# A gated activation bound by DMA: swapping the load and store queues, four-row activations, and the first load and first store cut into four transfers by partition

## The chip, the cores and the metric

The kernel runs on one core of one Trainium2 chip. DMA engines move the data between HBM, the chip's large memory, and SBUF, its on-chip memory, in which every tile here lies across 128 partitions. ACT (ScalarE) and DVE (VectorE) are the engines that compute here; SP only issues transfers here. A transfer *lands* when its data has arrived. The metric is device time in microseconds (us); a few rounds of the kernel before and of the other kernel alternate on one chip. All runs quoted with a ratio were in the fast state, with a granted clock of 1.0. A ratio is the mean time of one kernel's fast runs over the mean of the other's fast runs of the same rounds, so it is not quite the ratio of the medians quoted beside it.

## The reference

```python
# x: (32, 512, 2048) float32
x1, x2 = x[..., :1024], x[..., 1024:]
out = (x1 * (1 / (1 + np.exp(-x1)))) * x2        # (32, 512, 1024) float32
```

134.2 MB are read, 67.1 MB are written, and little is computed in between.

## The kernel before

There are 16 tiles of 1024 rows. A partition holds 8 consecutive rows of x, which are 64 KB in one piece in HBM, and 32 KB of output. Input tile `xt` and output tile `ot` have two buffers each. Loads are issued on ACT's queue, stores on SP's.

```python
K = 8; KC = 2
in_pool  = ctx.enter_context(tc.tile_pool(name="in_pool", bufs=2))
out_pool = ctx.enter_context(tc.tile_pool(name="out_pool", bufs=2))

def load(i):
    xt = in_pool.tile([P, K, in_cols], dt, name="xt")
    nc.scalar.dma_start(out=xt[:, :plan[i][1], :], in_=view(x_flat, i))
    loaded[i] = xt

load(0)                       # moved ahead of the first barrier
load(1)
for i in range(n_tiles):
    # ... xt, ov, ot, last
    for c in range(0, k, KC):
        # ot[c:ce] = Silu(xt[c:ce, :half]) on ACT
        # ot[c:ce] *= xt[c:ce, half:]      on DVE
        if last:
            nc.sync.dma_start(out=ov[:, c:ce, :], in_=ot[:, c:ce, :])
    if not last:
        nc.sync.dma_start(out=ov, in_=ot[:, :k, :])
    if i + 2 < n_tiles:
        load(i + 2)
```

## Time and profile before

| | before |
|---|---|
| time, median of 3 runs | 470.97 us (470.84 to 471.04) |
| span of the profiled run | 468.9 us |
| DVE busy, ACT busy | 142.3 us, 118.2 us |
| bytes moved, mean rate | 201.35 MB, 429 GB/s |

These are lines of the page of the kernel before: busy time of each engine with its share of the span; the DMA share in 40 slices (9 is 90% or more); the two DMA queues with packets, MB and share of the 16 DMA engines; and the chain of waits, by engine and by line.

```profile
DVE 142.3 (30%) x64; ACT 118.2 (25%) x65; POOL 0.2 (0%) x4
...
DMA  9899999999999998999999999999999989999998
...
q10 hardware_dynamic: 2304, 134.22, 66.4%
q1 hardware_dynamic: 2736, 67.11, 33.2%
...
DMA 80%; DVE 15%; ACT 3%; DVEq 0%; issue 0%
DMA xt<-in_x_dram 80%; DVE ot L92 15%; ACT ot L87 3%; DVEq L128 0%
```

No compute engine is busy for a third of the time, while DMA is busy in every slice: DMA is the bound. In the chain the DMA part is all loads (`xt<-in_x_dram`): a tile's compute starts when its load lands. The view of waits of the kernel before says the same (microseconds in total, times, longest):

```profile
ACT ot L87 <- DMA xt<-in_x_dram: 338.8, 16, 22.1
```

Two stretches of the kernel before, the start and the middle (columns: stretch, length, busy time of each engine, granted clock, DMA share, GB/s):

```profile
0.00:28.00 28.00, 4.18 (x2) 7.41 (x5) 0.20 (x4) 1.00 0.97 412
60.00:434.00 374.00, 115.65 (x52) 95.01 (x52) 0.00 (x0) 1.00 1.00 433
```

The trace holds a record of every DMA packet: start, duration, size, queue. It doesn't name the engine; the packets fall into sixteen chains, in each of which a packet starts where another ends, and a chain is taken for an engine. A load is 128 packets of 64 KB, eight for each of the 16 DMA engines; a store is 128 packets of 32 KB. In the steady part a load packet takes 2.418 us and a store packet 1.213 us, and each engine goes from one packet to the next without a gap (of 3696 steps between 60 and 434 us over 99% have none, and the longest is 0.32 us). 64 KB in 2.418 us is 27.1 GB/s an engine, or 434 GB/s for sixteen. The 433 GB/s that the view gives for the middle stretch agrees.

### The profile page before, as it was taken

The page shows a single profiled execution, that of the slowest core. Times are in us where ns is not written, and L with a number is a line of the kernel's source. Part 1 is how long each engine was busy: PE and PEld are TensorE (multiplying, and loading weights), DVE is VectorE, ACT ScalarE, POOL GpSimd, SP SyncE. Part 2 cuts the span into 40 slices and gives each one's busy share as a digit, 9 for nine tenths or more (in the row PEclk, how much of TensorE's full clock was granted, in tenths as well). Part 3 has the DMA queues.
Part 4 walks back from the last instruction along what each step waited for, and adds up shares of the span by engine and source line. Part 5 has one row for each costly group of instructions (what it writes and reads, how often), then busy time and mean ns, then how long its engine had stood idle before and what let it go on. Part 6 is the DMA issues. An engine that isn't in the chain of part 4 may idle for free.

```text
span 468.9 us, 269 instructions
## 1 busy us (share of the span) xinstructions
DVE 142.3 (30%) x64; ACT 118.2 (25%) x65; POOL 0.2 (0%) x4
## 2 busy tenths in 40 slices
DVE  0070705106061160601507025070250702407034
ACT  1142406023060330603206032060420604106051
POOL 0000000000000000000000000000000000000000
DMA  9899999999999998999999999999999989999998
GB/s 431 375 447 403 447 447 447 403 419 431 447 447 403 447 492 363 442 492 391 458 403 439 456 447 403 409 442 447 447 403 444 467 386 447 442 419 481 400 409 354
DMA packets 5042, 201.35 MB, mean 429 GB/s; under 512 B 560, under 2 KB 560, under 8 KB 560
## 3 DMA queue, kind: packets, MB, share of 16 engines
q10 hardware_dynamic: 2304, 134.22, 66.4%
q1 hardware_dynamic: 2736, 67.11, 33.2%
q14 instruction: 2, 0.02, 0.0%
HBM read 134.22 MB, written 67.11 MB: 429 GB/s over the span
## 4 chain that ended last, share of the span: by engine, by line
DMA 80%; DVE 15%; ACT 3%; DVEq 0%; issue 0%
DMA xt<-in_x_dram 80%; DVE ot L92 15%; ACT ot L87 3%; DVEq L128 0%
## 5 line engine op out<-in xcount | busy, mean ns | idle before, releaser
L92 DVE TENSOR_TENSOR ot<-ot,xt 128x2048 f32<-128x2048 f32 x64 | 142.3, 2286 | 319.5 <-ACT ot L87 319.5
L87 ACT ACTIVATE ot<-xt 128x2048 f32<-128x2048 f32 x64 | 116.9, 1897 | 338.8 <-DMA xt<-in_x_dram 338.8
L87 ACT ACT_TABLE_LOAD x1 | 1.3, 1283 | 1.3 <-PEq L117 1.3
L117 POOL MEMSET const-uint8-127<- 128x1 uint8 x1 | 0.1, 102 | 0.0
L117 POOL MEMSET const-bfloat16-1.0<- 128x1 bf16 x1 | 0.1, 101 | 0.0
L117 POOL MEMSET const-float32-0.0<- 128x1 f32 x1 | 0.1, 98 | 0.2 <-issue 0.2
L117 POOL MEMSET const-float32-1.0<- 128x1 f32 x1 | 0.1, 98 | 0.0
## 6 DMA issues: line engine op xcount, KB each, us to landing
out_dram<-ot SPq DMA_DIRECT2D x15, 4096.0 KB, 39.8
out_dram<-ot SPq DMA_DIRECT2D x4, 1024.0 KB, 5.7
xt<-in_x_dram ACTq DMA_DIRECT2D x16, 47.1
```

The lines of the kernel that those rows point to most:

```text
L87: nc.scalar.activation(out=ot[:, c:ce, :], in_=xt[:, c:ce, :half], func=mybir.ActivationFunctionType.Silu,)
L92: nc.vector.tensor_mul(out=ot[:, c:ce, :], in0=ot[:, c:ce, :], in1=xt[:, c:ce, half:],)
L117: nc = _bacc.Bacc("TRN2", target_bir_lowering=False, num_devices=1)
```

## The change

The intent, as far as the code tells: start each DMA queue sooner by giving it a small first transfer (one partition for each DMA engine), and halve the number of ACT and DVE instructions.

```diff
-    K = 8
-    KC = 2
+    K = 8
+    KC = 4
+    KC_LAST = 2
+    STARTING = [slice(0, None, 8), slice(4, None, 8), slice(2, None, 4), slice(1, None, 2)]
...
+    def start_ring(queue, dst, src, split):
+        for ps in STARTING if split else [slice(None)]:
+            queue.dma_start(out=dst[ps], in_=src[ps])
...
-        nc.scalar.dma_start(out=xt[:, :plan[i][1], :], in_=view(x_flat, i))
+        start_ring(nc.sync, xt, view(x_flat, i), split=i == 0)
...
+        if i < n_tiles - 1:
+            for c in range(0, K, KC):
+                silu(ot, xt, c, c + KC)
+                mul(ot, xt, c, c + KC)
+            start_ring(nc.scalar, ov, ot, split=i == 0)
+            if i + 2 < n_tiles:
+                load(i + 2)
+            continue
+        # last tile: two rows at a time, each store issued two activations later, on nc.scalar
```

All four parts of the first load, instead of one load, are moved ahead of the first barrier.

More of the change, by code (lines that the diff above doesn't have):

```diff
@@ L6, with issue_ahead_of_the_first_barrier @@
 from concourse._compat import with_exitstack
-def issue_ahead_of_the_first_barrier(nc):
+def issue_ahead_of_the_first_barrier(nc, count):
     head, body = nc.main_func.blocks[:2]
-    load = next(ins for ins in body.instructions if type(ins).__name__ == "InstDMACopy")
+    loads = [ins for ins in body.instructions if type(ins).__name__ == "InstDMACopy"][:count]
     at = next(
         j for j, ins in enumerate(head.instructions)
-        if ins.engine == load.engine and type(ins).__name__ == "InstDrain"
+        if ins.engine == loads[0].engine and type(ins).__name__ == "InstDrain"
     )
-    body.instructions = [ins for ins in body.instructions if ins.name != load.name]
-    head.instructions = head.instructions[:at] + [load] + head.instructions[at:]
+    names = {ins.name for ins in loads}
+    body.instructions = [ins for ins in body.instructions if ins.name not in names]
+    head.instructions = head.instructions[:at] + loads + head.instructions[at:]
 @with_exitstack
@@ L63, in view @@
         return flat[row0:row0 + P * k].rearrange("(p k) d -> p k d", k=k)
-    nc.at_finalize(issue_ahead_of_the_first_barrier)
+    nc.at_finalize(lambda nc: issue_ahead_of_the_first_barrier(nc, len(STARTING)))
     ctx.enter_context(tc.manual_schedule())
+    def start_ring(queue, dst, src, split):
+        for ps in STARTING if split else [slice(None)]:
+            queue.dma_start(out=dst[ps], in_=src[ps])
     loaded = {}
@@ L73, in load, with silu, mul @@
         xt = in_pool.tile([P, K, in_cols], dt, name="xt")
-        nc.scalar.dma_start(out=xt[:, :plan[i][1], :], in_=view(x_flat, i))
+        start_ring(nc.sync, xt, view(x_flat, i), split=i == 0)
         loaded[i] = xt
+    def silu(ot, xt, c, ce):
+        nc.scalar.activation(
+            out=ot[:, c:ce, :],
+            in_=xt[:, c:ce, :half],
+            func=mybir.ActivationFunctionType.Silu,
+        )
+    def mul(ot, xt, c, ce):
+        nc.vector.tensor_mul(
+            out=ot[:, c:ce, :],
+            in0=ot[:, c:ce, :],
+            in1=xt[:, c:ce, half:],
+        )
     load(0)
@@ L79 @@
     for i in range(n_tiles):
-        k = plan[i][1]
         xt = loaded.pop(i)
-        last = i == n_tiles - 1
         ov = view(out_flat, i)
         ot = out_pool.tile([P, K, half], dt, name="ot")
-        for c in range(0, k, KC):
-            ce = min(c + KC, k)
-            nc.scalar.activation(
-                out=ot[:, c:ce, :],
-                in_=xt[:, c:ce, :half],
-                func=mybir.ActivationFunctionType.Silu,
-            )
-            nc.vector.tensor_mul(
-                out=ot[:, c:ce, :],
-                in0=ot[:, c:ce, :],
-                in1=xt[:, c:ce, half:],
-            )
-            if last:
-                nc.sync.dma_start(out=ov[:, c:ce, :], in_=ot[:, c:ce, :])
-        if not last:
-            nc.sync.dma_start(out=ov, in_=ot[:, :k, :])
-        if i + 2 < n_tiles:
-            load(i + 2)
+        if i < n_tiles - 1:
[6 more added lines that the diff above has]
+            continue
+        cuts = list(range(0, K, KC_LAST))
+        for n, c in enumerate(cuts + [None, None]):
+            if c is not None:
+                silu(ot, xt, c, c + KC_LAST)
+                mul(ot, xt, c, c + KC_LAST)
+            if n >= 2:
+                b = cuts[n - 2]
+                nc.scalar.dma_start(out=ov[:, b:b + KC_LAST, :], in_=ot[:, b:b + KC_LAST, :])
 _INS = ['x']
```

## The prediction

> **What bounds the kernel now.** The 16 DMA engines. The engine table gives DVE 142.3 us and ACT 118.2 us of 468.9; the slices show DMA busy at 8 to 9 tenths throughout; the DMA view gives 201.35 MB at a mean of 429 GB/s. [...] (a 64 KB load packet takes 2.418 us on one engine, so 434 for sixteen). In the packet records the engines work back to back from 1.14–1.84 us to 466.8–467.6 us, with no gap over 0.4 us. At 434 GB/s the bytes need 464 us (an estimate), so only about 5 us is not steady transfer:
> - start: the first packet begins 1.0 us after the first load is issued at 0.13 us, and the 16 first packets take 2.5–3.4 us, mostly 0.6–0.9 too long;
> - first store: issued at 32.75 us, and at 35.65–36.0 us every engine has one load packet of 3.2–3.4 us, 0.85 us too long. No later store shows this. Both are the first use of a queue;
> - end: 1.3 us from the last packet to the last instruction.
>
> **What the change does.**
> 1. Split first load and first store: the first transfer is 16 partitions, one descriptor per engine instead of eight. [...] Estimate: 0.5–1.0 us off the start and 0.4–0.8 off the first store, on all engines at once, so on the critical path. Cost: three more issues each (0.33–0.38 us in the timeline), hidden behind the 2.4 us packets.
> 2. Loads on SP, stores on ACT: same engines, same bytes. At most 0.1 us at the start (SP's first instruction is at 0.00 us, ACT's at 0.13).
> 3. Four-row activations: from ACT 1.9 us and DVE 2.29 us for two rows, a tile takes about 12.5 us instead of 10.8. Store and next load are issued 1.7 us later, but a load is already queued (8.4 MB, over 19 us), so DMA doesn't idle: worth 0. Fewer fixed costs on ACT and DVE: worth 0.
> 4. Last tile: stores issued two activations later, on ACT. After the last load lands (451.0 us) DMA works 16.1 us more, of which 9.7 us are the last tile's stores; 6.4 us of older stores cover the wait for the first. The last store still goes when the last multiply ends, with about 3 us of slack. Worth 0.
>
> **Predicted.** 470.97 − 1.3 = 469.7 us, range 468.7 to 472.5. Faster by over 2%: 0.01; within 2%: 0.93; slower by over 2%: 0.06.
>
> **What would show it.** The first 64 KB packets take 2.4–2.7 us; no packet near 35 us takes over 3 us; total DMA bytes and the 2.418 us steady packet unchanged; ACT and DVE busy time fall by several us without effect; DMA is still about 80% of the chain of waits; the span falls by 1 to 1.6 us.
>
> **What would make it wrong.** The partitions of the split transfers. [...] If sixteen engines take one partition each, [...] packets of about 4.8 us (store: 2.4), some 5 us lost on the load and 2.5 on the store; if the bigger parts collide as well, up to 19 and 10 us, slower by over 2%. No run here shows it yet; I take it to be unlikely[...]. Also, if the stall is a fixed cost of waking a queue, the split gains nothing: 471.0.

No number of the sum is cut: 470.97 − 1.3 = 469.7 us. The 1.3 us is about the middle of the two estimates of step 1 taken together (0.5–1.0 and 0.4–0.8 us), and these come from the first packets and the load packet at the first store, 0.6–0.9 and 0.85 us too long in the trace. That a smaller first transfer shortens them was an assumption and not shown. In the risk, 4.8 and 2.4 us are an estimate, twice the 2.418 and 1.213 us of the trace.

## The result, and the profile after

| | before | after |
|---|---|---|
| time, median of 6 runs | 471.0 us (470.71 to 471.12) | 483.85 us (483.66 to 484.75) |
| ratio, 95% interval | | 1.0278 (1.0265 to 1.0291) |
| span of the profiled run | 468.9 us | 482.1 us |
| DVE busy, ACT busy | 142.3 us, 118.2 us | 140.3 us, 115.4 us |

The change makes the kernel 2.8% slower. The same lines of the page of the changed kernel:

```profile
DVE 140.3 (29%) x34; ACT 115.4 (24%) x35; POOL 0.2 (0%) x4
...
DMA  9999999999999999999999999999999999999997
...
q1 hardware_dynamic: 2352, 134.22, 66.9%
q10 hardware_dynamic: 2784, 67.11, 32.4%
...
DMA 77%; DVE 14%; ACT 6%; DVEq 0%; ACTq 0%; SPq 0%; issue 0%
DMA out_dram<-ot 71%; DVE ot L95 14%; ACT ot L88 6%; DMA xt<-in_x_dram 5%; DVEq L149 0%; ACTq L78 0%; SPq L78 0%; ACT L88 0%; ACTq L88 0%
```

Here is a trap for the reader: DMA is as busy as before and moves the same bytes, so the busy shares show nothing wrong. What changed is how long the same packets take, and what the chain is made of. Its DMA part is now stores (`out_dram<-ot` 71%), where it was loads. The view of waits of the changed kernel:

```profile
ACT ot L88 <- DMA out_dram<-ot: 314.4, 14, 23.3
ACT L88 <- DMA xt<-in_x_dram: 27.3, 1, 27.3
ACT ot L88 <- DMA xt<-in_x_dram: 12.1, 1, 12.1
```

ACT waits 14 times for a store, because the output buffer it wants to write is still being stored when its input has landed. The same two stretches of the changed kernel:

```profile
0.00:28.00 28.00, 0.00 (x0) 0.74 (x1) 0.20 (x4) 1.00 0.98 337
60.00:434.00 374.00, 105.26 (x25) 85.47 (x24) 0.00 (x0) 1.00 1.01 427
```

So there are two losses, both at a DMA share of about 1: the first 28 us move 337 GB/s instead of 412, and the middle moves 427 instead of 433. The packet records say where. The mean load packet goes from 2.430 to 2.519 us; with 128 of them on each engine that is 11.4 us. Of the time above 2.418 us, 5.5 us an engine lie in the first load (before: 0.6) and 7.4 us after 60 us (before: 0.0). Most of the rest of the 13.2 us is imbalance: the engines finish between 476.98 and 480.96 us instead of between 466.81 and 467.62, and the slowest counts.

The first three packets of one engine of each kernel (start, duration in us; then the range of all sixteen engines):

```
before, first load:  1.14 3.15 | 4.29 2.42 | 6.70 2.42    first packets 2.47 to 3.44, then 2.42
after,  first load:  1.38 4.29 | 5.67 4.95 | 10.62 3.28   first packets 4.29 to 5.29, second 4.94 to 4.96, third 2.66 to 3.28, then 2.42
```

The two 16-partition transfers run at half rate (4.94 to 4.96 us for the second packet, against 2.42). Tile 0 lands at 27.17 us instead of 21.86.

The middle loss is spread over all tiles. Number a load's eight packets on an engine L0 to L7. From the third tile on, L1 is on average 0.16 us and L2 0.32 us too long, all others together about 0.05. The sequence of packets on one engine, near 200 us (`s` is a store packet, `#` a packet of 4 bytes that takes 9 ns, the number is ns above 2418):

```
before:  ... L4 s L5 # L6 s L7 s # s L0 s L1 s L2 ...
after:   ... L6 s L7 s # s L0 # L1 s L2+384 s L3 s L4 ...
```

Each engine has one `#` at the end of each transfer: the two queues hold 560 of them in the kernel before (35 transfers on 16 engines) and 656 in the changed one (41 transfers). In these records loads and stores alternate packet by packet, and a `#` stands in the sequence like a packet of its queue: between 60 and 434 us of the kernel before, 3680 of 3696 pairs of neighbours on an engine change the queue if the `#` is counted, and 2864 of 3280 if it isn't. So beside a store's `#` two loads follow each other, and beside a load's `#` two stores. Before, the store's `#` comes first and the load's 7.3 us later. After, the load's comes first and the store's 3.6 us later. The order of the two endings has flipped, and it stays so for the rest of the run.

### The profile page after: what moved, and what is told of

It reads as the page before. It is cut to its first block, busy times and chain, and to the rows that moved or that the text cites. A ratio compares the mean times of both kernels' runs of the same rounds, so it can differ in the third digit from the quotient of the medians.

```text
span 482.1 us, 219 instructions
## 1 busy us (share of the span) xinstructions
DVE 140.3 (29%) x34; ACT 115.4 (24%) x35; POOL 0.2 (0%) x4
## 4 chain that ended last, share of the span: by engine, by line
DMA 77%; DVE 14%; ACT 6%; DVEq 0%; ACTq 0%; SPq 0%; issue 0%
DMA out_dram<-ot 71%; DVE ot L95 14%; ACT ot L88 6%; DMA xt<-in_x_dram 5%; DVEq L149 0%; ACTq L78 0%; SPq L78 0%; ACT L88 0%; ACTq L88 0%
## 5 line engine op out<-in xcount | busy, mean ns | idle before, releaser
L95 DVE TENSOR_TENSOR ot<-ot,xt 128x4096 f32<-128x4096 f32 (+1 forms) x34 | 140.3, 4170 | 332.4 <-ACT ot L88 332.4
L88 ACT ACTIVATE ot<-xt 128x4096 f32<-128x4096 f32 (+1 forms) x34 | 114.1, 3407 | 326.5 <-DMA out_dram<-ot 314.4
```

What stands on the lines that cost most here:

```text
L88: nc.scalar.activation(out=ot[:, c:ce, :], in_=xt[:, c:ce, :half], func=mybir.ActivationFunctionType.Silu,)
L95: nc.vector.tensor_mul(out=ot[:, c:ce, :], in0=ot[:, c:ce, :], in1=xt[:, c:ce, half:],)
```

## The experiments

Fifteen kernels ran, in four groups, each beside the kernel before (medians 471.41, 471.37, 470.91 and 471.35 us in turn). All but three gave the right result. Executions of the runs with slow loads differ by up to 5 us (o from 480.04 to 485.06); why was not looked into.

The main theory had two parts by the end. The **collision theory**: in the 16-partition transfers some partitions that are moved at the same moment slow each other. The **order theory**: load packets are slow in every tile when the stores of a tile end after the next load has landed. The rivals were the distance of the rows in HBM, small transfers as such, the swap of the queues, the uneven engines that the split leaves, and the split store in itself.

### One part at a time

**a_load_split**: the kernel before with the load split alone (all four parts ahead of the first barrier, as in the changed kernel).

```diff
-        nc.scalar.dma_start(out=xt[:, :plan[i][1], :], in_=view(x_flat, i))
+        for ps in STARTING if i == 0 else [slice(None)]:
+            nc.scalar.dma_start(out=xt[ps], in_=view(x_flat, i)[ps])
```

> The kernel before with only its first load split in four (still on ACT). Collision theory: the two 16-partition transfers of the first load run at half rate, so tile 0 lands about 5.3 us later than before's 21.9 us, and that cost is there whatever else is changed: about 476 us from this alone. Spread theory for the other 7.5 us of the loss: the split leaves the 16 DMA engines 0.7 us apart instead of 0.35, and that spread grows and slows later loads; then this run loses them too and takes 480 to 484 us, with the spread at a landing growing from 0.7 to over 4 us. Phase theory: the slow loads come from where the first store's packets fall between the load packets; here compute and store start relative to the load packets about as before, so about 476 us and a spread that stays under 1.5 us.

Measured 475.17 us, ratio 1.0082 (1.0067 to 1.0097). Tile 0 landed at 27.4 us; the load packets after 60 us were all at 2.42 us, although the engines were 0.7 to 1.6 us apart. So the load split costs about 4 us, and engines as uneven as these don't by themselves slow the later loads. The split wins a little back: the stall at the first store, 0.9 us on each engine, is gone here. Why is open.

**b_store_split**: the kernel before with the store split alone.

```diff
-            nc.sync.dma_start(out=ov, in_=ot[:, :k, :])
+            for ps in STARTING if i == 0 else [slice(None)]:
+                nc.sync.dma_start(out=ov[ps], in_=ot[ps])
```

> The kernel before with only its first store split in four (still on SP). In the changed kernel the first store's packets took 1.21 to 1.58 us against 1.21, and no load packet near it stalled by 0.85 us as in the kernel before. Start-of-queue theory: this run loses the 0.85 us stall and is 0.5 to 0.9 us faster than before, about 470.3 us. Collision theory applied to stores: [...] store packets of about 2.4 us, 2 to 10 us slower. Phase theory: if the earlier start of store packets shifts the store tiles against the load tiles by a slot, later loads may slow by some us.

The 2.4 us for the collision is an estimate, twice the 1.213 us of a store packet.

Measured 470.95 us, ratio 0.9994 (0.9977 to 1.0011): the same. The load packet at the first store took 3.35 to 3.48 us, as against 3.18 to 3.42 before. So the stall doesn't shrink with the size of the first store, and step 1 of the prediction fails here. Stores and loads now end together (the store 0.01 us later), where the stores ended 7.3 us earlier before. The three added transfers put three more `#` into the store queue of each engine; if a load packet of 2.418 us goes beside each, that makes 7.3 us (an estimate). The view of waits:

```profile
ACT ot L88 <- DMA out_dram<-ot: 302.8, 14, 21.8
```

**c_no_split**: the changed kernel with `STARTING = [slice(None)]`, so neither is split.

> The changed kernel with neither transfer split: loads on SP, stores on ACT, four-row activations, later stores in the last tile. Collision theory with spread theory: no collision, no spread, so the time of before, 470 to 472 us. Queue theory (the swap of the two queues slows the later loads): about 478 us, loads of over 2.5 us in every tile. Phase theory: the first store comes 1.7 us later, so the store tiles may lie one slot (3.6 us) nearer to the load tiles; if so some loads in every tile are slow and it takes 472 to 479 us, and then the four-row run on the kernel before must show the same.

Measured 471.27 us, ratio 1.0003 (0.9985 to 1.0020): the same. Stores end 3.6 us before the next load. The swap of queues and the later stores of the last tile cost nothing.

**d_four_rows**: the kernel before with four-row activations in all tiles but the last (`kc = KC if last else 4`).

> The kernel before with four-row activations in all tiles but the last, nothing else. Queue theory and spread theory: as before, 471 us within 0.5. Phase theory: the store tiles come 1.7 us later against the load tiles; if the landing of a store moves from 7.3 us to about 3.6 us before the next load's landing, slow loads (over 2.5 us) appear in every tile and the time is 472 to 479 us.

Measured 471.38 us, ratio 1.0001 (0.9985 to 1.0017): the same. Stores end 3.6 us before the next load here too: the stores did move nearer, as expected, but no load was slow. Moving nearer isn't enough.

### Which split goes with which loss

**e_load_whole**: the changed kernel with `split=False` for the load. **f_store_whole**: the changed kernel with `split=False` for the store.

> The changed kernel with its first load in one transfer, the first store still in four. So far: splitting the load alone costs 4.2 us, swap and four rows alone nothing, splitting the store alone nothing; the changed kernel lost 12.9. In packet slots, the stores of a tile ended 2 slots before the next load's landing (before), 1 slot (four rows), 0 slots (store split), and by the order of packets 1 slot after it (the changed kernel). Order theory: slow loads of over 2.5 us in every tile come when the stores end after the loads; here four rows and the store split act together, the stores should again end about 1 slot after the loads, and the run loses 5 to 8 us without the load split: 476 to 479 us. Spread theory: slow loads need the load split's unequal engines as well: about 471 us, no slow loads after 60 us.

> The changed kernel with its first store in one transfer, the first load still in four. Order theory: without the three extra semaphore turns of the store queue the stores end before the next load lands, no slow loads after 60 us, only the collision's 4 to 5.5 us: 475 to 476.5 us. Spread theory: the engines are apart by 0.7 us as after the load split, so slow loads may grow here, 478 to 484 us.

The semaphore turns of f's forecast are the `#` packets, of which the split store of e puts three more into the store queue of each engine.

e took 479.72 us, ratio 1.0202 (1.0160 to 1.0244), with 324 loads over 2.5 us after 60 us; f took 475.00 us, ratio 1.0082 (1.0067 to 1.0097), with one. The two losses add up: 0.82% and 2.02% against 2.78% for the changed kernel. The load split makes the first loss; the split store makes the second, but only together with four rows (b has the split store and no loss). The waits of e, then its two stretches:

```profile
ACT ot L88 <- DMA out_dram<-ot: 314.6, 14, 23.5
ACT ot L88 <- DMA xt<-in_x_dram: 34.3, 2, 19.7
```

```profile
0.00:28.00 28.00, 2.56 (x1) 7.49 (x3) 0.20 (x4) 1.00 0.98 412
60.00:434.00 374.00, 105.14 (x24) 88.93 (x25) 0.00 (x0) 1.00 1.00 426
```

And the stretches of f:

```profile
0.00:28.00 28.00, 0.00 (x0) 0.62 (x1) 0.20 (x4) 1.00 0.98 337
60.00:434.00 374.00, 110.88 (x27) 92.60 (x26) 0.00 (x0) 1.00 1.00 433
```

One run has the loss in the start alone (337), the other in the middle alone (426), and the changed kernel has both.

### The first loss: partitions or HBM rows

The rows that the first transfers read are 512 KB apart in HBM, so HBM could have been the cause as well as the set of partitions.

**g_rows_in_order**: a_load_split, but the four partition sets read consecutive blocks of rows, and the store of tile 0, in the same four sets, puts them back.

```diff
+    ROWS = [slice(0, 16), slice(16, 32), slice(32, 64), slice(64, 128)]
-            nc.scalar.dma_start(out=xt[ps], in_=view(x_flat, i)[ps])
+            nc.scalar.dma_start(out=xt[ps], in_=view(x_flat, i)[rs])      # rs from ROWS
...
+                nc.sync.dma_start(out=ov[rs], in_=ot[ps])                 # tile 0
```

> The kernel before with the first load in the same four partition sets, but each set reads a block of consecutive rows of HBM (tile 0's rows lie in other partitions, and its store, in the same four sets, puts them back). SBUF side unchanged, HBM pitch within the first two transfers 64 KB instead of 512 KB. [...] the first two packets of each engine still take 4.2 to 5.0 us and tile 0 lands at about 27.3 us. HBM pitch theory: packets of 2.4 to 3.2 us, tile 0 lands at 21.5 to 22.2 us.

The first figures are the collision theory's.

The second packets took 4.92 us and tile 0 landed at 27.1 us. The distance of the rows doesn't matter. The time, 486.18 us (ratio 1.0340), came as a surprise: with both splits the stores end 1.7 us after the loads in this run, and L1 is slow by 0.5 us on average. So it has the second loss too, without four rows and without the swap.

This run also bounds what the order explains. In its steady part 9 of the 16 engines have the sequence that all engines of b have (`L7 s # # L0 s L1`), and 7 have that of the changed kernel; the slow load is there on all sixteen. Near 198, 228 and 257 us there are exactly 16 slow loads, one an engine and all in flight at the same moment, each 0.5 to 0.8 us too long. So it is not the order on an engine by itself that slows its packets. It looks like one pause that all engines share, which comes when some of them end their stores late.

**h_every_7th**: the first load as seven transfers of every 7th partition and one of the last 16.

```diff
-    STARTING = [slice(0, None, 8), slice(4, None, 8), slice(2, None, 4), slice(1, None, 2)]
+    STARTING = [slice(j, 112, 7) for j in range(7)] + [slice(112, 128)]
```

> The kernel before with the first load as seven transfers of every 7th partition and one of the last 16 partitions, 16 partitions each. [...] in the first packets 4 engines take 4.2 to 5 us and 12 about 2.4 to 3.3 us; the last transfer is the slowest, up to 9.7 us a packet. HBM pitch theory (512 KB pitch is bad, a pitch of 448 KB and of 64 KB not): all of about the same, 2.4 to 3.3 us, tile 0 lands near 22 us.

The first figures are the collision theory's: the author took the first packets of four engines to collide and those of the other twelve not; no run had shown which partitions collide. The 9.7 us is an estimate, four times the 2.418 us of the trace.

Measured 491.57 us, ratio 1.0432. The last transfer took 7.1 to 8.7 us a packet and fits the collision forecast alone. The first didn't: all sixteen first packets took 3.6 to 5.4 us, not just four of them, and the next two transfers 4.6 to 4.9. The transfers overlap here, so no single set can be read cleanly from this run. That called for a run with each set by itself.

**i_sets_alone**: only test transfers, each set moved twice and awaited before the next (result wrong).

```python
for n, ((p0, p1, ps), (u0, u1, us)) in enumerate(LOADS):      # u: units of 64 KB in HBM
    for h, t in enumerate((a, b)):
        nc.sync.dma_start(out=t[p0:p1:ps, :], in_=unit[at + u0:at + u1:us, :])   # at: from n and h
    nc.vector.tensor_mul(out=mark[:, 0:1], in0=a[:, 0:1], in1=b[:, 0:1])         # waits for both
```

> Measures the disputed transfers by themselves; its result is wrong on purpose (no activation, only test transfers). Each test moves the same set of partitions twice (two tiles), 64 KB a partition, from HBM, and waits for both before the next; then seven sets the other way, 32 KB a partition. So far every 16-partition load was slow: every 8th partition 4.95 us a packet whether the HBM rows were 512 KB or 64 KB apart, every 7th 3.2 to 4.9 us. [...] packets of about 2.4 to 3.3 us [...] (all 128 partitions; every 4th of 32; partitions 0 and 64), twice that [...] (every 8th; every 4th of 64; partitions 0 and 32; partitions 0 and 1), four times [...] (the first 16, first 8, first 4). Rival, one descriptor per engine is slow in itself: every load with one partition per engine takes 4 to 5 us a packet, even partition 0 alone; 128 and 64 partitions 2.4 us. Rival, HBM: the first 16 partitions with rows 64 KB apart differ from the same with rows 512 KB apart.

The first figures are the collision theory's, an estimate: once, twice and four times the 2.42 us packet, for the sets in the brackets. The packet of the second transfer of each pair, median, and the time from the first issue of the pair to the mark after both landings, from the timeline:

| partitions | us a packet | first issue to mark, us |
|---|---|---|
| all 128; every 2nd; every 4th | 2.42 | not read (a fill of `b` lies between the issues); 22.54; 12.82 |
| every 8th (16), HBM rows 512 KB apart | 5.12 | 13.17 |
| every 8th (16), HBM rows 64 KB apart | 5.11 | 12.77 |
| every 4th of the first 64 (16) | 5.12 | 12.81 |
| the first 16, HBM rows 64 KB or 512 KB apart | 9.64 | 21.62; 21.29 |
| every 4th of 32, or of 64 to 96 (8) | 2.42 | 7.48; 7.62 |
| every 8th of the first 64 (8) | 5.13 | 12.50 |
| the first 8; the first 4 | 9.64 | 20.75; 20.58 |
| 0 and 1; 0 and 32 | 5.13; 4.82 | 11.98; 11.63 |
| 0 and 4; 0 and 64 | 2.50; 2.42 | 6.88; 7.43 |
| 0 alone: first packet; second, beside the run's first store | 2.46; 3.53 | 7.26 |

A packet takes 2.42 us, 2.1 times as long or 4.0 times as long. Every slow set of 16 or fewer holds partitions that are neighbours or 32 apart; no fast set of 8 or fewer does.

The timeline of this run shows two of these pairs, first every 8th partition, later (after the cut) every 4th (start, duration; the TENSOR_TENSOR marks the landing of both transfers):

```profile
59.42 0.63 SPq L67 DMA_DIRECT2D a<-in_x_dram  x1
60.11 0.57 SPq L67 DMA_DIRECT2D b<-in_x_dram  x1
72.59 0.16 DVE L68 TENSOR_TENSOR mark<-a,b 128x1 f32<-128x1 f32 x1 [13.20 <-DMA b<-in_x_dram]
...
142.02 0.50 SPq L67 DMA_DIRECT2D a<-in_x_dram  x1
142.57 0.59 SPq L67 DMA_DIRECT2D b<-in_x_dram  x1
154.84 0.16 DVE L68 TENSOR_TENSOR mark<-a,b 128x1 f32<-128x1 f32 x1 [12.85 <-DMA b<-in_x_dram]
```

The second pair moves twice the bytes in the same time. Partitions 0 and 32 against 0 and 64 settle it: the same number of bytes in two packets at a time, 4.82 us for the one pair, 2.42 for the other. (Their HBM rows are 2 and 4 MB apart; the rows of 0 and 1, which are slow too, are neighbours.) One partition for each engine is not slow in itself either (every 4th of 32, 2.42 us; 0 alone in its first packet, 2.46 us). A set of 16 without neighbours and without partitions 32 apart was not run. Sets of every 4th and every 2nd partition and all 128 hold such partitions too and are at full rate, 2.42 us; why is not shown, and neither is which engine takes which partition. Stores collide in the same way when alone: every 8th partition took mostly 1.9 to 2.5 us a packet in the first transfer and 2.2 to 3.1 in the second, against 1.21. In the changed kernel the first store's small sets, with load packets of 2.42 us between them on each engine, took only 1.21 to 1.58 us; why is not shown.

**k_load_32**: a_load_split with `STARTING = [slice(0, None, 4), slice(2, None, 4), slice(1, None, 2)]`: strided sets of 32 and 64 partitions only.

> The kernel before with the first load as 32, 32 and 64 partitions (every 4th, every 4th from 2, every 2nd from 1). In the load split of four, the 32 and 64 sets ran at 2.42 us a packet. If only 16-partition sets are slow: packets of 2.4 to 3.3 us, tile 0 lands at about 22 us, no stall of the loads near the first store (the load-split run had none), so 0 to 1 us faster than before: 470.0 to 471.0 us. [...]

Measured 471.85 us, ratio 1.0019 (1.0006 to 1.0032). The collision is gone (first packets 2.4 to 3.6 us, then 2.42; tile 0 at 22.4 us). Nothing is gained either: the stall at the first store is back (3.26 to 3.69 us).

### The second loss: order or split

**j_late_first_store**: d_four_rows with the activations of tile 0 done twice (`for _ in range(2 if i == 0 else 1)`), no split. **l_store_in_two**: e_load_whole with the first store in two (`slice(0, None, 2)` and `slice(1, None, 2)`).

> The four-row run with the activations of tile 0 done twice (same result, no transfer split): the first store is issued 6.4 us later, at about 40.8 us. Order theory: the stores, which ended 1 slot before the next load's landing in the four-row run, now end after it; slow loads (index 1 and 2 of each tile, total 0.4 to 0.7 us an engine and tile) and 477 to 480 us. Rival, the split store itself (its extra semaphores or partial sets) causes the slow loads: no split here, so 471 to 472 us.

> The load-whole run (479.7 us) with the first store in two transfers (every 2nd partition) instead of four. [...] Order theory: the stores of a tile end at or before the next load's landing, no slow loads, 471 to 472 us. Rival, any partition-split first store with this order of queues causes them: 475 to 480 us.

l has two `#` fewer than e in the store queue of each engine; that the stores then lag less was the reason for l, and they do (−2.3 us against +3.6, table below).

j took 472.67 us (1.0051), with no slow load after 60 us. My delay missed its aim: load 2 was held back as much as the store, both queues started together at about 41 us, and stores and loads end together (0.01 us apart). It therefore says only that a late store in itself brings no slow loads; most of the 1.8 us that it lost is an idle gap of 0.8 to 1.5 us on every DMA engine before 41.9 us. l took 471.11 us (1.0003) with one slow load. Its stores end 2.3 us before the load by the last engine, but that is the doing of one engine: on the other fifteen both end together.

**m_store_held**: c_no_split with only the store of tile 0 held back until the first activation of tile 1 is issued. Load 2 keeps its place, and nothing is split.

```diff
             for c in range(0, K, KC):
                 silu(ot, xt, c, c + KC)
+                if i == 1 and c == 0:
+                    start_ring(nc.scalar, *first_store, split=False)
                 mul(ot, xt, c, c + KC)
-            start_ring(nc.scalar, ov, ot, split=i == 0)
+            if i == 0:
+                first_store = (ov, ot)
+            else:
+                start_ring(nc.scalar, ov, ot, split=False)
```

> The no-split run with the store of tile 0 issued only after the first activation of tile 1, at about 46 us instead of 34, while the load of tile 2 keeps its place; no transfer is split anywhere. Order theory: the store queue starts 2 to 3 load packets after load 2 has begun, so from then on the stores of a tile end 2 to 4 us or more after the next load's landing, activations wait for a store's landing, and loads of index 1 and 2 are slow in every tile: 476 to 485 us, 300 or more loads over 2.5 us. Rival, the split store itself is the cause: 471 to 473 us, no slow loads after 60 us.

Measured 479.15 us, ratio 1.0162 (1.0145 to 1.0180), 328 slow loads after 60 us, mostly L1 and L2. The store was issued at 41.3 us, not at 46. Its waits and its middle stretch:

```profile
ACT ot L88 <- DMA out_dram<-ot: 315.8, 14, 25.5
```

```profile
60.00:434.00 374.00, 106.01 (x25) 90.01 (x26) 0.00 (x0) 1.00 1.00 427
```

Against c_no_split, the run that it was made from:

```profile
ACT ot L88 <- DMA xt<-in_x_dram: 340.8, 16, 22.0
```

```profile
60.00:434.00 374.00, 113.89 (x26) 92.59 (x26) 0.00 (x0) 1.00 1.00 433
```

One store issued 7 us later, once, at the start, costs 7.8 us against the kernel before (medians). The second loss needs no split at all. With j it makes a close pair: the first store at 41 us in both, but load 2 ahead of it only in m.

**o_other_rows**: e_load_whole with each store sent to the place of the tile five further on (`view(out_flat, (i + 5) % n_tiles)`). **p_short_multiply**: e_load_whole with the multiply cut to 8 columns from the third tile on (`mul(..., half if i < 2 else 8)`). Their outputs are wrong, which doesn't matter for the times.

> The load-whole run (479.7 us) with the store of each tile sent to the place of the tile five further on (result wrong on purpose), so the HBM addresses written beside a given load differ by 20 MB. Order theory in which only the sequence of the transfers counts: still 478 to 481 us with about 350 slow loads of index 1 and 2. Rival, a clash of HBM addresses between loads and the stores beside them: fewer or other loads are slow, 471 to 476 us.

> The load-whole run (479.7 us) with the multiply of every whole tile from the third on cut to 8 of 1024 columns (result wrong on purpose): stores and loads are issued about 4.6 us sooner after the landing and VectorE hardly touches SBUF. Order theory in which only the sequence at the queues counts: the sequence is kept by the queues, which are never empty, so 478 to 481 us and slow loads of index 1 and 2 as before. Rival, the slow loads come from the time of issue or from VectorE's traffic: they move to other indexes or vanish, 471 to 476 us.

o took 481.97 us (1.0231) with 327 slow loads, p 481.11 us (1.0195) with 349, again L1 and L2. So it isn't a clash of the HBM addresses of a load and the stores beside it, at least not one that a shift of 20 MB alters; nor is it VectorE's traffic, or the time at which the next transfers are issued. ScalarE's traffic was not varied. The traces speak against it: in the kernel before, 416 load packets after 60 us overlap an activation by over 2 us and none is slow, and in the changed kernel 36 of the 327 slow loads overlap no activation.

All runs side by side, with the time from the landing of a load to the end of the store nearest to it (last engine, median of 150 to 440 us), and the loads over 2.5 us after 60 us:

| run | store end minus load landing, us | slow loads of 2048 |
|---|---|---|
| before, a | −7.3 | 0 |
| h | −5.3, later −4.6 | 0 |
| k | −5.1 | 0 |
| c, d, f | −3.6 | 0, 0, 1 |
| l | −2.3 | 1 |
| j, b | 0.0 | 0 |
| g | +1.7 | 268 |
| after, e, m | +3.6 | 327, 324, 328 |
| o, p | from +2.0 and +2.5, shrinking to 0.0 and +0.4 | 327, 349 |

Every run in which the stores end later for most of this stretch has hundreds of slow loads; no other run has more than one. The column goes by the last engine, which hides something in o and p: on 15 of their 16 engines the store ends 3.6 us after the load all along, and a single engine that runs behind brings the difference to 0.0. In b and j, with 0.0 as well, the ends coincide on every engine.

## Why the prediction was wrong

**What bounds the kernel** was read rightly. The DMA engines work back to back in both kernels, and the bytes are the same.

**Step 1, the split, was wrong, and on the term that it left out.** It gave "0.5–1.0 us off the start and 0.4–0.8 off the first store". At the start, the first two packets took 4.3 to 5.3 us instead of 2.4 to 2.7, so the split cost 5.5 us an engine where 0.6 had been lost. At the first store, b showed that the stall stays (3.35 to 3.48 us) when the first store is split. The stall is missing in the changed kernel, but it is missing as well in a and f, whose store is whole.

**The risk was named with the right size and the wrong odds.** "Packets of about 4.8 us … some 5 us lost on the load" is what happened (4.95 us, 5.3 us later landing). The 4.8 us is twice the 2.418 us of the trace, an estimate. "I take it to be unlikely" rested on nothing measured. For the store the figure of 2.4 us is right alone but not beside loads.

**Step 3 failed in the sentence "DMA doesn't idle: worth 0", and step 1 in counting only the issues as the cost of the split store.** DMA indeed never idles; its packets get slower. Taken alone, four rows (d) are worth 0, and so is the split store (b). But the later first store and the three added `#` of the split store together shift the stores against the loads until the stores end last, and with that order go about 8 us (e). The argument treated the queues as a pool of bytes, in which order can't count.

**Step 2**, the swap, **and step 4**, the late stores of the last tile, were right: with four rows they took 471.27 us against 471.41 (c).

**What stays open.** The collision is shown (i: partitions 0 and 32 take 4.82 us, 0 and 64 2.42). That the time of one first store decides over the second loss is shown by m, and that the loss goes with stores that end last by m and the table. What in the chip slows the loads in that order is not shown: HBM addresses (by 20 MB), VectorE's traffic and the time of issue are ruled out by o and p, and uneven engines alone by h, where they are 2.7 us apart and no load is slow. By g the order on each engine is not enough; in the changed kernel too, 14 or 15 of the slow loads of a tile are in flight at one moment, over most of the run. What that pause is stays open. In that order ACT also waits for a store in place of a load; b waits for stores too and loses nothing, so that wait alone isn't the cause. More output buffers were not tried; smaller tiles would have changed the transfers under test and were not tried either. No run beats the kernel before beyond the noise.

## What to carry to other kernels

When a transfer is cut by partition, time each part by itself: of 128 partitions, every 8th (16) took 5.12 us a packet and the first 16 took 9.64, while every 4th, every 2nd and all took 2.42 (i). (To cut along another dimension may avoid the question; it wasn't tried here.) In a kernel bound by DMA, look at the durations of packets and not only at busy shares: here the load packet went from 2.430 to 2.519 us in the mean, and the DMA share of the middle was 1.00 and 1.01. And where loads and stores alternate on two queues, check which ends first in a tile: here one first store issued 7 us later set that order for the whole run and cost 7.8 us (m).
